# A hybrid encoder trunk on one core: first loads, kept activation sums, an earlier turn and a reshared scaling

## The chip, the core and the metric

The kernel runs on one core of a Trainium2 chip. The metric is the time of one execution in device microseconds (us), taken as the median of several runs. TensorE does the matrix products, VectorE (DVE in the profile), ScalarE (ACT) and GpSimd (POOL) the rest, and SyncE (SP), ACT and POOL issue the DMAs.

## The reference

All tensors are float32. There are 256 positions, the model width is 2048, and there is one layer. Cut to what matters:

```python
def mixer_block(x, ...):
    h = rms_norm(x, g_norm)
    proj = h @ w_in                       # 2048 x 9216: u, v | q, k, v | gates A, B
    uv, qkv, gates = jnp.split(proj, ...)
    y_a = gmlp_branch(uv, ...)            # gelu, LayerNorm of v, spatial mixing of 128 positions, times u
    y_b = neighbourhood_attn(q, k, v, rpb)
    g_a, g_b = jnp.split(jax.nn.sigmoid(gates), 2, axis=-1)
    merged = g_a * (y_a @ w_branch[:GM_WIDTH]) + g_b * (y_b @ w_branch[GM_WIDTH:])
    return x + merged @ w_out

def conv_ffn(x, ...):
    up = rms_norm(x, g_norm) @ w_up       # 2048 x 11008
    up = (pad[:, :t] * conv_k[0] + pad[:, 1:t + 1] * conv_k[1] + pad[:, 2:t + 2] * conv_k[2] + conv_b)
    gate, val = jnp.split(up, 2, axis=-1)
    return x + (jax.nn.silu(gate) * val) @ w_down   # 5504 x 2048

out = rms_norm(conv_ffn(mixer_block(x, ...), ...), norm_final)
```

## The kernel before, in words

**Split products.** Every factor is split in two parts of the type fp32r: a high part (ACT copies it, L151 for weights, tile `whi`) and the rest (DVE subtracts, L152, tile `wlo`). A product is then three matmuls, high by high, low by high and high by low (`triple`, L287 to L291). The activations are split likewise: `x_split` (L493) multiplies the transposed input `xr` by the first norm's gain `gmix`, ACT the high part (L495) and DVE the low one (L496).

**Pieces.** The weights come in pieces of 512 KB, loaded by SP in the order in which they are used, five ahead (`load_to`, L112), and split up to three ahead (`split_to`, L140; four tiles each of `whi` and `wlo`). `begin(i)` (L178) stands ahead of the products of piece `i`: it loads, splits, and runs the tasks that `at(i, f)` has filed under that number. In the first nine pieces the tasks run ahead of the splits and `SPLIT_TO` says how far is split; later the splits come first. A task's instructions stand at that place in each engine's queue, and each engine runs as far ahead as its waits let it.

**Wide groups and seven-product pairs.** A wide group (`run_wide`, L340) makes 1024 output columns for both halves of the positions: four PSUM banks `C[t][c]`, 16 pieces of one 128-row chunk of the weights each. A plain piece is four triples, 12 matmuls. A pair of pieces named in the group's `QUADS` is done by seven products in place of eight, 21 matmuls: DVE adds up blocks of the weights (`weight_sums`, L321, three pieces ahead), ACT and DVE split these (L334, L335, two pieces ahead), and like sums of the activations are needed too (`act_sums`, L300, and `act_sums_split`, L311). Such pairs need four more banks `P`, from the group's first pair to its last, which DVE then reads (`post_sums`); `add_sums` joins both at the group's end. There are eight banks, and a group that takes one waits for the last reader of what was in it.

**Order.** The wide groups are: `g_v` (the gMLP's v, pieces 0 to 15, its order of chunks in `V_ORDER`), `g_va` (attention's v, 16 to 31), then `g_u`, the q and k groups with the first halves of the gates, the branch products (`g_branch`), the second halves of the gates `g_gw[0]` and `g_gw[1]` (pieces 128 to 159), four branch groups `g_m2`, the out projection `g_o` (two wide groups), the up projection and the down projection `g_dn` (two). The first groups' activation sums are made from `xr` (L305), those of the gates again from the split parts (L307). After the second branch's product of a quarter `j`, `ev_branch` (L859) multiplies by the gates (L863) and adds (L866), and `turn_m(j)` (L878) transposes the result: eight TensorE transposes (L885), then ACT and DVE split it (L470, L475).

**Start and end.** Before the first matmuls TensorE runs `WAKE` transposes (L440). The norm's factor is made by `rstd` (L444): the sum (L1187), DVE (L449), a square root on ACT (L450), and five DVE operations. At the end `finish` (L1054) handles one bank of the last group at a time: it adds the residual (L1021), ACT squares it and sums (L1024), DVE multiplies by the last gain (L1061); after the second bank of a half the factor `r` times `e` is made (L1066 to L1072) and `write` (L1074) scales 2048 columns in five parts on DVE (L1083) and ACT (L1081) and stores them in five DMAs (L1087).

Of the kernel before, what the change touches and what calls it, by code (L numbers as in the profile page):

```python
# [8 lines left out]
F32 = mybir.dt.float32  # L9
# [48 lines left out]
Y_GAP = 224  # L58
DOWN_PAIRS = (3, 5, 7, 9, 10, 12, 14, 16, 17, 19)
# [4 lines left out]
def trunk_kernel(ctx, tc, x, x_t, vecs, w_in, ln_g, ln_b, w_st, b_s, rpb, w_branch, w_out, w_up, w_down,  # L64
# [200 lines left out]
    def wide(src, row0, order, c0, acts, quads, room, done, sums=None, odd=None, stored=None, split_room=None):  # L265
        n0 = plan_wide(src, row0, order, c0)
        boxes = {}
        for n, q in enumerate(quads):
            i = n0 + 2 * q
            own = odd if odd and n % 2 else split_room or room  # L270
# [40 lines left out]
    def act_sums_split(box, room, name):  # L311
        w = box.pop("w")
        o = room(name, F32R)
        nc.scalar.activation(o[:, 0], w[:, 1], AF.Copy)
        nc.vector.tensor_sub(o[:, 1], w[:, 1], o[:, 0].bitcast(F32))
        box["s"] = sums_of(o)
# [23 lines left out]
    def run_wide(g, tail=0):  # L340
        kind, n0, order, acts, quads, boxes, done = g
        n1 = n0 + len(order)
        P = C = None

        def x_of(k, t):
            a = acts(k)
            return a[:, 0, t * 128:(t + 1) * 128], a[:, 1, t * 128:(t + 1) * 128]

        def plain(i, t, c):
            h, l = split_t[i]  # L350
            triple(C[t][c], x_of(order[i - n0], t), h[:, c], l[:, c], i == n0, i == n1 - 1)

        for i in range(n0, n1 - tail):
            begin(i)
            q, r = divmod(i - n0, 2)
            if C is None:
                c = [bank() for _ in range(4)]
                C = [c[:2], c[2:]]
            if q not in quads:
                for t, c in ((0, 0), (0, 1), (1, 0), (1, 1)) if i > 1 else ((0, 0), (1, 0), (0, 1), (1, 1)):  # L360
                    plain(i, t, c)
                split_t.pop(i)
                continue
            st, sp = q == quads[0], q == quads[-1]
            k, k1 = order[2 * q:2 * q + 2]
            if r == 0:
                if st:
                    P = [bank() for _ in range(4)]
                (h0, l0), (h1, l1) = split_t[i], split_t[i + 1]
                triple(P[0], x_of(k, 0), h0[:, 0], l0[:, 0], st, sp)  # L370
                triple(C[0][0], x_of(k1, 0), h1[:, 0], l1[:, 0], False, False)
                triple(C[0][1], boxes[q]["acts"]["s"][3], h1[:, 1], l1[:, 1], False, False)
# [7 lines left out]
            triple(C[1][0], x_of(k1, 1), *W[4], False, False)  # L380
# [26 lines left out]
    xr = xin.tile([128, KD, T], F32, name="xr")  # L407
# [5 lines left out]
    def load_xt(k, n, queue=None):  # L413
        (queue or nc.sync).dma_start(xr[:, k:k + n], x_t[:, k:k + n])

    gmix = const.tile([128, KD], F32)
    gffn = const.tile([128, KD], F32)
    ck = const.tile([128, 4, 2 * NF], F32)
    nc.scalar.dma_start(gmix, vecs[:, 0:KD])
    load_xt(1, 1, nc.scalar)  # L420

    def load_late():
        nc.sync.dma_start(gffn, vecs[:, KD:2 * KD])
        nc.sync.dma_start(ck.rearrange("p a b -> p (a b)"), vecs[:, 2 * KD:])
# [19 lines left out]
    def rstd(name, ssum, n, eps):  # L444
        w = ssum.shape[-1]
        a = const.tile([128, w], F32, name=name + "_a")
        r = const.tile([128, w], F32, name=name + "_r")
        s = const.tile([128, w], F32, name=name + "_s")
        nc.vector.tensor_scalar(a, ssum, 1.0 / n, float(eps), op0=OP.mult, op1=OP.add)  # L449
        nc.scalar.activation(s, a, AF.Sqrt)  # L450
        nc.vector.reciprocal(r, s)
# [166 lines left out]

    def mix(g):
        p = bank()  # L620
# [7 lines left out]
        split_plain(y, yT[g])  # L628
# [230 lines left out]
    def ev_branch(br, j):  # L859
        def done(ps, i):  # L860
# [3 lines left out]
            if br == 1:  # L864
                for t in range(NT):
                    nc.vector.tensor_add(g[:, t, :], g[:, t, :], mg[0, j][:, t, :])  # L866
                at(i + 2, lambda: turn_m(j))
# [186 lines left out]
    def finish(ps, t, c):  # L1054
# [7 lines left out]
        if c == 0:  # L1062
            if t:
                fin["out"]()
            return
        a, r, q, e, pt, both = (const.tile([128, 1], F32, name=f"{n}3{t}") for n in "arqepb")  # L1066
        nc.vector.tensor_scalar(pt, fin["ss"][:, t, 2:3], 1.0 / D, fin["part"][:, t:t + 1], op0=OP.mult, op1=OP.add)
        nc.vector.tensor_scalar(a, fin["ss"][:, t, 3:4], 1.0 / D, pt, op0=OP.mult, op1=OP.add)
        nc.scalar.activation(q, a, AF.Sqrt)
        nc.vector.reciprocal(r, q)  # L1070
        nc.vector.scalar_tensor_tensor(e, r, r, a, op0=OP.mult, op1=OP.mult)
        nc.vector.tensor_scalar(e, e, -0.5, 1.5, op0=OP.mult, op1=OP.add)  # L1072

        def write():  # L1074
            on_act = (3,) if t else (1, 3)
            cuts = (0, 256, 768, 1024, 1536, 2048)
            for n in (0, 1, 2, 3, 4):
                v = x2[:, t, cuts[n]:cuts[n + 1]]
                u = y[:, n - 3] if n > 2 else v
                if n in on_act:  # L1080
                    nc.scalar.activation(v, u, AF.Copy, scale=both)  # L1081
                else:
                    nc.vector.tensor_scalar(v, u, r, e, op0=OP.mult, op1=OP.mult)  # L1083
                if n == 0:
                    nc.vector.tensor_mul(both, r, e)
            for n in (0, 1, 2, 3, 4):
                (nc.scalar if n == 3 else nc.sync).dma_start(out[0, t * 128:(t + 1) * 128, cuts[n]:cuts[n + 1]],  # L1087
                                                             x2[:, t, cuts[n]:cuts[n + 1]])
# [15 lines left out]
    def odd_room(name, dt):  # L1104
        return s_room["odd"].tile([128, 2, 512], dt, name=name)

    first_sums = {2 * q: {} for q, _, _ in X_SUMS}
    g_v = wide(w_in2, 0, V_ORDER, V0, xt, V_QUADS, first_room, (ev_v_sums, ev_v), first_sums,
               odd_room)
    g_va = wide(w_in2, 0, VA_ORDER, VA0, xt, VA_QUADS, first_room, (ev_va_sums, ev_va), first_sums)  # L1110
    for n, (q, i, j) in enumerate(X_SUMS):
        sum_acts_at(i, j, first_sums[2 * q], lambda q=q: q,
                    lambda name, dt, i=i: first_room("s2" if name == "f" and i < 9 else name, dt), f"s{n}", True)
# [13 lines left out]
    x_sums, m_sums = ({2 * q: {} for q in qs} for qs in (GATE_PAIRS, OUT_PAIRS))  # L1127
# [5 lines left out]
    for n, q in enumerate(GATE_PAIRS):  # L1133
        i = g_gw[0][1] - 3 + 3 * n
        sum_acts_at(i, i + 1, x_sums[2 * q], lambda q=q: x_pairs[q], sums_room, f"s{n}")
    for n, q in enumerate(OUT_PAIRS):
        i = g_m2[0][1] + 2 + 3 * n
# [29 lines left out]
    dram = keep("dram", space=bass.MemoryType.DRAM)  # L1167
# [9 lines left out]
    for c, i in X_TURN[1:]:  # L1177
        at(i, lambda c=c: x_chunk(c))

    xsq = const.tile([128, NT, 4], F32)  # L1180
# [3 lines left out]

    def x_norm():
        s = const.tile([128, NT], F32, name="ss1")
        nc.vector.tensor_reduce(s, xsq, axis=AX.X, op=OP.add)  # L1187
        r = rstd("n1", s, D, RMS_EPS)
        st1["r"] = r
# [31 lines left out]
    s_room["odd"], odd_st = pool("odd")  # L1221
    at(g_v[1] + 15, odd_st.close)
# [119 lines left out]
```

## Time and profile before

| what | value |
|---|---|
| median of three runs | 1307.59 us (1307.04 to 1307.76) |
| profiled execution, its own time | 1307.19 us |
| its span in the profile | 1305.4 us |
| granted TensorE clock, mean | 0.998 |
| TensorE busy with matmuls | 1292.6 us of the span |
| DVE, ACT, POOL busy | 1082.7, 780.6, 104.7 us |
| moved by DMA | 277.19 MB |

The span runs from the first to the last instruction of the program; 1.8 us of the execution's own time lie around it. Times in the views count from the start of the span. A matmul's end is modelled and the next one starts before it, so what a matmul costs is read from start to start; a line such as "x3" holds several instructions in a row.

### The profile page before, as it was taken

The page shows a single profiled execution, that of the slowest core. Times are in us where ns is not written, and L with a number is a line of the kernel's source. Part 1 is how long each engine was busy: PE and PEld are TensorE (multiplying, and loading weights), DVE is VectorE, ACT ScalarE, POOL GpSimd, SP SyncE. Part 2 cuts the span into 40 slices and gives each one's busy share as a digit, 9 for nine tenths or more (in the row PEclk, how much of TensorE's full clock was granted, in tenths as well). Part 3 has the DMA queues.
Part 4 walks back from the last instruction along what each step waited for, and adds up shares of the span by engine and source line. Part 5 has one row for each costly group of instructions (what it writes and reads, how often), then busy time and mean ns, then how long its engine had stood idle before and what let it go on. Part 6 is the DMA issues. An engine that isn't in the chain of part 4 may idle for free.

```text
span 1305.4 us, 19280 instructions
## 1 busy us (share of the span) xinstructions
PE 1292.6 (99%) x6706; PEld 1102.7 (84%) x6706; DVE 1082.7 (83%) x1634; ACT 780.6 (60%) x1158; POOL 104.7 (8%) x206
## 2 busy tenths in 40 slices
PE   9999999999999999999999999999999999999997
PEld 7888888888888888888888888888888888888885
DVE  7997777677689978897777878787888889999997
ACT  7766476666655644566556556565555656565563
POOL 0006405413000000000000000000000000000000
PEclk9999999999999999999999999999999999999999
DMA  9779656556556656665566666666666758876772
GB/s 357 245 245 267 183 166 214 174 171 194 178 171 203 219 182 242 208 210 164 176 198 206 184 211 195 216 195 214 190 210 199 217 157 290 291 266 226 273 285 104
DMA packets 174225, 277.19 MB, mean 212 GB/s; under 512 B 13488, under 2 KB 121904, under 8 KB 174128
## 3 DMA queue, kind: packets, MB, share of 16 engines
q1 hardware_dynamic: 165520, 252.28, 59.9%
q0 software_dynamic: 8032, 23.03, 5.3%
q8 instruction: 52, 0.85, 0.3%
q10 hardware_dynamic: 576, 0.66, 0.1%
q14 instruction: 45, 0.37, 0.1%
HBM read 266.48 MB, written 7.34 MB: 210 GB/s over the span
## 4 chain that ended last, share of the span: by engine, by line
PE 96%; DVE 2%; ACT 1%; DMA 1%; issue 0%; SPq 0%; ACTq 0%; DVEq 0%
PE bank L203 31%; PE bank L207 16%; PE bank L291 11%; PE bank L289 11%; PE bank L290 11%; PE bank L231 5%; PE bank L233 4%; PE bank L232 4%; DMA wraw<-in_w_in_dram 1%; PE bank L756 1%; DVE wlo L152 0%; PE bank L806 0%; PE bank L622 0%; PE bank L796 0%; PE bank L957 0%
## 5 line engine op out<-in xcount | busy, mean ns | idle before, releaser
L152 DVE TENSOR_TENSOR wlo<-wraw,whi 128x1024 fp32r<-128x1024 f32 (+1 forms) x472 | 545.3, 1169 | 171.7 <-ACT whi L151 93.8
L151 ACT ACTIVATE whi<-wraw 128x1024 fp32r<-128x1024 f32 (+1 forms) x472 | 469.7, 1009 | 207.0 <-PE bank L290 81.3
L203 PE MATMUL bank<-h,whi 128*128 128x512 f32 x1760 | 425.5, 392 | 0.0
L203 PEld LDWEIGHTS bank<-h,whi 128*128 128x128 f32 x1760 | 322.1, 188 | 61.7
L207 PEld LDWEIGHTS bank<-h,wlo 128*128 128x128 f32 x1760 | 225.9, 191 | 8.8
L207 PE MATMUL bank<-h,wlo 128*128 128x256 f32 x1760 | 228.6, 283 | 0.0
L983 ACT ACTIVATE tc<-ta,ck 128x256 f32<-128x256 f32 x86 | 47.1, 595 | 117.7 <-DVE ta L981 117.7
L291 PE MATMUL bank<-wlo,a 128*128 128x512 f32 x224 | 87.3, 390 | 0.0
L289 PE MATMUL bank<-whi,a 128*128 128x512 f32 x224 | 87.2, 389 | 0.0
L290 PE MATMUL bank<-whi,a 128*128 128x512 f32 x224 | 87.2, 389 | 0.0
L290 PE MATMUL bank<-whi,h 128*128 128x512 f32 x210 | 81.9, 390 | 0.8 <-DVE h L496 0.8
L289 PE MATMUL bank<-whi,h 128*128 128x512 f32 x210 | 82.4, 392 | 0.2
L291 PE MATMUL bank<-wlo,h 128*128 128x512 f32 x210 | 82.0, 390 | 0.6 <-DVE wlo L152 0.5
L334 ACT ACTIVATE h<-h 128x1024 fp32r<-128x1024 f32 x40 | 40.2, 1053 | 35.0 <-DVE h L326 35.0
L986 DVE SCALAR_TENSOR_TENSOR tc<-ta,ck,tc 128x255 f32<-128x255 f32 x86 | 41.5, 482 | 14.4 <-ACT tc L983 14.4
L231 PE MATMUL bank<-whi,y 128*128 128x512 f32 x128 | 50.5, 394 | 0.0
L231 PE MATMUL bank<-whi,h 128*128 128x512 f32 x128 | 50.4, 394 | 0.0
L233 PE MATMUL bank<-wlo,h 128*128 128x512 f32 x128 | 49.9, 390 | 0.0
L233 PE MATMUL bank<-wlo,y 128*128 128x512 f32 x128 | 49.9, 390 | 0.0
L232 PE MATMUL bank<-whi,h 128*128 128x512 f32 x128 | 49.9, 389 | 0.0
L232 PE MATMUL bank<-whi,y 128*128 128x512 f32 x128 | 49.8, 389 | 0.0
L291 PEld LDWEIGHTS bank<-wlo,a 128*128 128x128 f32 x224 | 42.0, 188 | 9.1 <-DVE wlo L152 0.3
(290 smaller groups left out, 1800.4 us busy)
## 6 DMA issues: line engine op xcount, KB each, us to landing
wraw<-in_w_up_dram SPq DMA_DIRECT2D x336, 256.0 KB, 3.3
wraw<-in_w_in_dram SPq DMA_DIRECT2D x111, 512.0 KB, 4.3
wraw<-in_w_down_dram SPq DMA_DIRECT2D x86, 512.0 KB, 5.4
wraw<-in_w_in_dram SPq DMA_DIRECT2D x66, 256.0 KB, 3.1
wraw<-in_w_branch_dram SPq DMA_DIRECT2D x32, 512.0 KB, 4.5
wraw<-in_w_out_dram SPq DMA_DIRECT2D x32, 512.0 KB, 4.2
h<-sums POOLq DMA_DIRECT2D x20, 512.0 KB, 6.7
sums<-so POOLq DMA_DIRECT2D x10, 512.0 KB, 5.5
```

The source lines that it names most:

```text
L151: nc.scalar.activation(h[:, k, :m], w[:, k, :m], AF.Copy)
L152: nc.vector.tensor_sub(l[:, k, :m], w[:, k, :m], h[:, k, :m].bitcast(F32))
L203: nc.tensor.matmul(p, h[:, k - k0, b * 128:(b + 1) * 128], acts(k), start=k == 0, stop=k == nk - 1)
L207: nc.tensor.matmul(p[:, :T], l[:, k - k0, b * 128:(b + 1) * 128], acts(k)[:, 0, :], start=False, stop=False)
L231: nc.tensor.matmul(p, xh, h[:, kk, :m], start=st, stop=False)
L232: nc.tensor.matmul(p, xl, h[:, kk, :m], start=False, stop=False)
L233: nc.tensor.matmul(p, xh, l[:, kk, :m], start=False, stop=sp)
L289: nc.tensor.matmul(p, xh, h, start=st, stop=False)
L290: nc.tensor.matmul(p, xl, h, start=False, stop=False)
L291: nc.tensor.matmul(p, xh, l, start=False, stop=sp)
L983: nc.scalar.activation(v, u, AF.Identity, scale=ck[:, 1, ch:ch + 1], bias=ck[:, 3, ch:ch + 1])
L986: nc.vector.scalar_tensor_tensor(v[:, 1:], u[:, :T - 1], ck[:, 0, ch:ch + 1], v[:, 1:], op0=OP.mult, op1=OP.add)
```

## The change

- **First loads.** `gmix` is laid in front of the transposed input in memory and comes with its chunk 0 in one DMA on ACT's queue, with chunk 1 behind it; SP's queue begins with the weights. Chunks 6 and 7 come in a DMA each, ahead of pieces 2 and 3; chunks 2 and 3 come three pieces later than before (and are split two pieces later), chunks 4, 5 and 12 to 15 one. DVE takes the high part of chunk 0. Chunk 6 is split ahead of the weights of piece 2, chunk 7 ahead of those of piece 3. There are 14 `WAKE` transposes in place of 17.
- **First group.** `g_v` has one seven-product pair (pieces 10 and 11) in place of two; the room `odd` goes away. The sums of chunks 2 and 3 are made at pieces 5 and 6 in place of 3 and 4, those of 4 and 5 at 12 and 13 in place of 6 and 9. The norm's sum and root (`x_root`) go ahead of the other tasks of piece 17, the rest (`inverse`) stays behind them.
- **Gates.** `g_gw[0]` has four seven-product pairs, the first at its first piece, `g_gw[1]` three as before, at other places. The activation sums of three pairs are kept: POOL stores the tiles of the first groups to memory (`keep_sums`) and loads them again from four pieces ahead of `g_gw[0]` (`kept_sums`); the fourth is made from the split parts. `first()` marks the first product of a bank, since a pair can now open a group.
- **Turns.** `turn_m(1)` moves from piece 2 of `g_gw[0]` to piece 2 of `g_gw[1]`, `turn_m(3)` from piece 2 of the out projection to its piece 1. The sums for the out projection are made one piece later. In `mix` the split of a result goes to the next piece.
- **End.** The part of the sum that is known after a half's first bank (`p`) is made there, ACT takes the root with the scale and `p` in one instruction, and each half is scaled in four parts (DVE 768 and 512 columns, ACT 512 and 256) and stored in three DMAs.

```diff
-WAKE = 17
-V_QUADS, V_ORDER = ((5, 6), (0, 1, 6, 7, 8, 9, 10, 11, 12, 13, 2, 3, 4, 5, 14, 15))
+WAKE = 14
+V_QUADS, V_ORDER = ((5,), (0, 1, 6, 7, 8, 9, 10, 11, 12, 13, 2, 3, 4, 5, 14, 15))
-X_TURN = ((0, 0), (3, 1), (1, 2), (4, 2), (5, 3), (2, 4), (6, 6), (7, 9))
-SPLIT_TO = (3, 4, 4, 7, 8, 8, 11, 12, 12)
+X_TURN = ((0, 0), (3, 1), (4, 2), (5, 3), (1, 4), (2, 5), (6, 6), (7, 9))
+SPLIT_TO = (2, 4, 4, 7, 8, 8, 11, 12, 12)
-X_SUMS = ((1, 3, 4), (2, 6, 9), (6, 18, 19))
-GATE_PAIRS = (2, 4, 6)
-GATE_QUADS = ((2, 4, 6), (1, 3, 5))
-GATE_ORDER = (tuple(range(16)), (0, 1, 4, 5, 2, 3, 8, 9, 6, 7, 12, 13, 10, 11, 14, 15))
+X_SUMS = ((1, 5, 6), (2, 12, 13), (6, 18, 19))
+GATE_KEPT, GATE_MADE = (1, 2, 6), 4
+GATE_QUADS = ((0, 2, 4, 6), (2, 4, 6))
+GATE_ORDER = ((2, 3, 0, 1, 4, 5, 6, 7, 12, 13, 10, 11, 8, 9, 14, 15), (0, 1, 6, 7, 2, 3, 10, 11, 4, 5, 14, 15, 12, 13, 8, 9))
+KEEP_AT = (22, 25, 29)
...
-    nc.scalar.dma_start(gmix, vecs[:, 0:KD])
+    load_xt(0, 1, nc.scalar)
     load_xt(1, 1, nc.scalar)
...
     def x_split(k):
         a, g = xT[k], gmix[:, k:k + 1]
-        nc.scalar.activation(a[:, 0, :], xr[:, k], AF.Copy, scale=g)
+        if k:
+            nc.scalar.activation(a[:, 0, :], xr[:, k], AF.Copy, scale=g)
+        else:
+            nc.vector.tensor_scalar(a[:, 0, :], xr[:, k], g, None, op0=OP.mult)
...
-        split_plain(y, yT[g])
+        gm_pool["last"] = lambda: split_plain(y, yT[g])
+        at(cur[0] + 1, end_mix)
...
-                at(i + 2, lambda: turn_m(j))
+                at(i + 1 if j == 3 else g_gw[1][1] + 2 if j == 1 else i + 2, lambda: turn_m(j))
...
-        nc.vector.tensor_scalar(pt, fin["ss"][:, t, 2:3], 1.0 / D, fin["part"][:, t:t + 1], op0=OP.mult, op1=OP.add)
-        nc.vector.tensor_scalar(a, fin["ss"][:, t, 3:4], 1.0 / D, pt, op0=OP.mult, op1=OP.add)
-        nc.scalar.activation(q, a, AF.Sqrt)
+        nc.scalar.activation(q, ss, AF.Sqrt, scale=1.0 / D, bias=pt)
+        nc.vector.tensor_scalar(a, ss, 1.0 / D, pt, op0=OP.mult, op1=OP.add)
...
+        nc.vector.tensor_mul(both, r, e)
...
+            for u, w in ((v[:, :768], v[:, :768]), (y[:, 1], v[:, 1536:])):
+                nc.vector.tensor_scalar(w, u, r, e, op0=OP.mult, op1=OP.mult)
+            for u, w in ((y[:, 0], v[:, 1024:1536]), (v[:, 768:1024], v[:, 768:1024])):
+                nc.scalar.activation(w, u, AF.Copy, scale=both)
+            nc.sync.dma_start(o[:, :768], v[:, :768])
+            nc.sync.dma_start(o[:, 1536:], v[:, 1536:])
+            nc.scalar.dma_start(o[:, 768:1536], v[:, 768:1536])
...
+    def x_root():
+        s = const.tile([128, NT], F32, name="ss1")
+        nc.vector.tensor_reduce(s, xsq, axis=AX.X, op=OP.add)
+        st1["root"] = root("n1", s, D, RMS_EPS)
+    def x_norm():
+        st1["r"] = inverse(*st1["root"])
+    at(NORM_AT, x_root)
...
+    def keep_sums(q):
+        nc.gpsimd.dma_start(x_kept[q], first_sums[2 * q]["tile"].bitcast(F32))
+    def kept_sums(n, q):
+        o = sums_room(f"s{n}", F32R)
+        nc.gpsimd.dma_start(o.bitcast(F32), x_kept[q])
+        x_sums[2 * q]["s"] = sums_of(o)
+    for n, q in enumerate(GATE_KEPT):
+        at(KEEP_AT[n], lambda q=q: keep_sums(q))
+        at(g_gw[0][1] - 4 + n, lambda n=n, q=q: kept_sums(n, q))
+    sum_acts_at(g_gw[0][1] - 1, g_gw[0][1] + 1, x_sums[2 * GATE_MADE], lambda: x_pairs[GATE_MADE], sums_room, "s3")
...
-        i = g_m2[0][1] + 2 + 3 * n
+        i = g_m2[0][1] + 3 + 3 * n
...
-    preload[0] = [lambda: load_xt(0, 1)]
-    for n, (c, _) in enumerate(X_TURN[1:]):
-        preload[n + 2] = [lambda c=c: load_xt(2 * c, 2)]
+    first_chunk = X_TURN[1][0]
+    preload[2] = [lambda: load_xt(2 * first_chunk, 1)]
+    preload[3] = [lambda: load_xt(2 * first_chunk + 1, 1)]
+    for n, (c, _) in enumerate(X_TURN[2:]):
+        preload.setdefault(n + 4, []).append(lambda c=c: load_xt(2 * c, 2))
...
+    at(1, lambda: x_split(2 * first_chunk))
+    at(1, lambda: split_to(3))
+    at(1, lambda: x_split(2 * first_chunk + 1))
```

More of the change, by code (lines that the diff above doesn't have):

```diff
@@ L260, in run_group, with wide @@
             done(ps, b)
-    def wide(src, row0, order, c0, acts, quads, room, done, sums=None, odd=None, stored=None, split_room=None):
+    def wide(src, row0, order, c0, acts, quads, room, done, sums=None, stored=None, split_room=None):
         n0 = plan_wide(src, row0, order, c0)
         boxes = {}
-        for n, q in enumerate(quads):
+        for q in quads:
             i = n0 + 2 * q
-            own = odd if odd and n % 2 else split_room or room
+            own = split_room or room
             whole[i] = whole[i + 1] = None
@@ L343, in run_wide, with first @@
         P = C = None
+        begun = set()
+        def first(t, c):
+            new = (t, c) not in begun
+            begun.add((t, c))
+            return new
         def x_of(k, t):
@@ L350, in plain @@
             h, l = split_t[i]
-            triple(C[t][c], x_of(order[i - n0], t), h[:, c], l[:, c], i == n0, i == n1 - 1)
+            triple(C[t][c], x_of(order[i - n0], t), h[:, c], l[:, c], first(t, c), i == n1 - 1)
         for i in range(n0, n1 - tail):
@@ L370, in run_wide @@
                 triple(P[0], x_of(k, 0), h0[:, 0], l0[:, 0], st, sp)
[L371 to L372 removed]
+                triple(C[0][0], x_of(k1, 0), h1[:, 0], l1[:, 0], first(0, 0), False)
+                triple(C[0][1], boxes[q]["acts"]["s"][3], h1[:, 1], l1[:, 1], first(0, 1), False)
                 split_t.pop(i)
@@ L379, in run_wide @@
             triple(P[2], S[2], *W[2], st, sp)
-            triple(C[1][0], x_of(k1, 1), *W[4], False, False)
+            triple(C[1][0], x_of(k1, 1), *W[4], first(1, 0), False)
             if sp:
@@ L617, in combine, with end_mix @@
         return outs
+    def end_mix():
+        gm_pool.pop("last", lambda: None)()
     def mix(g):
+        end_mix()
         p = bank()
@@ L1072, in finish @@
         nc.vector.tensor_scalar(e, e, -0.5, 1.5, op0=OP.mult, op1=OP.add)
+        nc.vector.tensor_mul(both, r, e)
         def write():
[L1075 to L1088, printed above, removed]
+            v = x2[:, t]
+            o = out[0, t * 128:(t + 1) * 128]
+            for u, w in ((v[:, :768], v[:, :768]), (y[:, 1], v[:, 1536:])):
[5 more added lines that the diff above has]
+            nc.scalar.dma_start(o[:, 768:1536], v[:, 768:1536])
         if t:
```

62 lines of the change are left out of this document (29 added, 33 removed).

## The prediction

> **What bounds the kernel now.** I read the page first, then TensorE's waits, then the timelines around each of them.
>
> ```profile
> span 1305.4 us, 19280 instructions
> PE 1292.6 (99%) x6706; PEld 1102.7 (84%) x6706; DVE 1082.7 (83%) x1634; ACT 780.6 (60%) x1158; POOL 104.7 (8%) x206
> PE 96%; DVE 2%; ACT 1%; DMA 1%; issue 0%; SPq 0%; ACTq 0%; DVEq 0%
> PE bank L289 <- DVE m L475: 0.8, 1, 0.8
> PE bank L290 <- DVE h L496: 0.8, 1, 0.8
> PE bank L291 <- DVE wlo L152: 0.5, 1, 0.5
> 507.92 0.39 PE L289 MATMUL bank<-whi,m 128*128 128x512 f32 x1
> 510.63 0.39 PE L289 MATMUL bank<-whi,m 128*128 128x512 f32 x1
> ```
>
> TensorE sets the time: 96% of the chain, and few waits. The last two rows are the starts of two neighbouring plain pieces: 2.71 us for 12 matmuls, 0.226 us from start to start. So a change pays where it takes matmuls away, where it takes one of the few stalls away, or at the two ends. A view counts only the idle time after a matmul's modelled end; I take a stall as start to start less 0.23.
>
> Matmuls: `g_v` loses a seven-product pair (three matmuls more, 3 x 0.226 = 0.68 us), `g_gw[0]` gains one (0.68 less). Together nothing. What is left are stalls.
>
> **First loads.**
>
> ```profile
> 1.37 3.89 PE L440 MATMUL bank<-ident 128*128 128x128 f32 x17 [1.37 <-POOL ident masks.py:199]
> 4.64 0.63 ACT L151 ACTIVATE whi<-wraw 128x512 fp32r<-128x512 f32 x1 [0.93 <-DMA wraw<-in_w_in_dram]
> 5.33 0.76 PE L289 MATMUL bank<-whi,h 128*128 128x512 f32 x1
> 6.16 0.40 PE L291 MATMUL bank<-wlo,h 128*128 128x512 f32 x1
> 9.99 1.06 ACT L151 ACTIVATE whi<-wraw 128x1024 fp32r<-128x1024 f32 x1 [2.15 <-DMA wraw<-in_w_in_dram]
> 11.08 1.23 DVE L152 TENSOR_TENSOR wlo<-wraw,whi 128x1024 fp32r<-128x1024 f32 x1 [2.44 <-ACT whi L151]
> 12.22 0.88 DVE L496 SCALAR_TENSOR_TENSOR h<-xr,gmix,h 128x256 fp32r<-128x256 f32 x2
> 13.10 0.40 PE L291 MATMUL bank<-wlo,h 128*128 128x512 f32 x1
> 18.37 0.39 PE L290 MATMUL bank<-whi,h 128*128 128x512 f32 x1
> 18.85 0.50 PE L291 MATMUL bank<-wlo,h 128*128 128x512 f32 x1
> 6.00:21.00 15.00, 14.00 (x59) 10.66 (x58) 12.14 (x23) 12.32 (x22) 0.00 (x0) 1.00 1.03 401
> ```
>
> Two things make the stalls: piece 2's weights land at 9.99 (the ACT row is released by the DMA), and chunk 6 is split behind them (12.22), so that the second product starts late and the third, at 13.10, later still. At 18.37 a third product waits 0.25 for `wlo`, held up on DVE by the early activation sums.
>
> After: the weights are first on SP's queue, and less goes ahead of them. The first matmul followed 0.69 behind the ACT row at 4.64; the chunk that was ahead of them now takes turns with them from ACT's queue, where another followed it before; some 110 KB less by then, at 300 to 400 GB/s, is 0.35, so it comes at about 4.98. Up to piece 2's weights there are 128 KB less (one chunk in place of two), at the 401 GB/s of the last row 0.33; with the gain's many tiny rows gone I take 0.44: they land at 9.55. Then `whi` to 10.6, `wlo` (1.23) to 11.9, third product at 11.95. Without any wait it would come 26 products and some 0.5 for the slow first ones behind 4.98, at 11.4, so a stall of 0.55 stays, where the weights now come last and not the chunk. Against 13.10 that is 1.15. The stall at 18.37, 0.25 and 0.11 in the next start, goes too: `wlo` of piece 4 is, by the same durations, ready at 16.95 and wanted at 17.4. Sum 1.5. Bounds: weights no earlier than before, 1.0; no stall left at all, 2.1. DVE's high part of chunk 0 costs nothing, since DVE waits there anyway until 5.3; if that cover were gone, 0.4.
>
> [...]
>
> **The first group's end.**
>
> ```profile
> 54.57 0.69 DVE L324 TENSOR_TENSOR y<-wraw 128x512 f32<-128x512 f32 x1
> 57.49 0.20 ACT L450 ACTIVATE n_s<-n_a 128x2 f32<-128x2 f32 x1 [4.36 <-DVE n_a L449]
> 61.08 0.91 ACT L305 ACTIVATE y<-xr,gmix 128x256 f32<-128x256 f32 x2 [0.53 <-DVE y L335]
> 64.45 1.04 ACT L151 ACTIVATE whi<-wraw 128x1024 fp32r<-128x1024 f32 x1
> 65.54 0.50 PE L289 MATMUL bank<-whi,h 128*128 128x512 f32 x1
> 65.52 1.22 DVE L152 TENSOR_TENSOR wlo<-wraw,whi 128x1024 fp32r<-128x1024 f32 x1 [2.29 <-ACT whi L151]
> 66.80 0.50 PE L291 MATMUL bank<-wlo,h 128*128 128x512 f32 x1 [0.53 <-DVE wlo L152]
> ```
>
> Piece 22 starts at 65.54 and its third product only at 66.80 in place of 65.99: with the slower starts around it 0.9 us. Read back: `wlo` waits for `whi`, ACT is late since it waited 4.36 us for `n_a`, and DVE made that behind four weight sums (from 54.57, 2.5 us). After, `x_root` goes ahead of those sums, and the pair that is gone leaves DVE nothing to catch up. TensorE is by now 1.5 - 0.68 = 0.82 earlier, and so is the half `whi` of piece 20, which waits for it: 51.8 to 52.4. From there on DVE: `wlo` to 53.05, root 0.4, weight sums to 55.95, inverse 0.95, `wlo` 1.15, first L335 1.15, so L305 on ACT can start at 59.2 (before: 61.08); from it to the end of the gelu 3.4 as before (61.08 to 64.45), then `whi` 1.05 and `wlo` 1.2: done at 64.9, wanted at 65.2. Gain 0.8, with only 0.3 to spare; bounds 0.3 and 0.9. The kept sums' stores are POOL's and wait only for their tiles, so they run at about 24, 40 and 65 us, not at 22, 25 and 29 pieces; nothing is queued behind them on POOL that is due before 100 us. As DMA they delay later weights by 1.3 us each, which lie 1.5 us or more ahead of their use.
>
> **Gates.**
>
> ```profile
> 361.69 0.69 PE L806 MATMUL bank<-pT,vw 128*64 128x64 f32 x16
> 371.66 1.23 DVE L152 TENSOR_TENSOR wlo<-wraw,whi 128x1024 fp32r<-128x1024 f32 x1 [0.56 <-ACT whi L151]
> 379.19 1.35 DVE L863 TENSOR_TENSOR g<-bank,g 128x512 f32<-128x512 f32 x2
> 379.65 0.39 PE L289 MATMUL bank<-whi,h 128*128 128x512 f32 x1
> h<-sums POOLq DMA_DIRECT2D x20, 512.0 KB, 6.7
> ```
>
> `g_gw[0]` starts at 379.65, without a stall. Now a pair opens it. Weight sums (four adds, 54.57 to 57.1 above, 2.5) and their split (two of 1.2) come ahead of the branch's L863 at 379.19, less half a `wlo` and one 0.6 split: L863 moves some 3 us to 382.2, the first bank free at 382.9. The group now takes all eight banks in its first two pieces. In what order, the wait at 517.95 (below) shows: there the fourth matrix `P[3]`, third to be written, started when two of the four L475 (517.05 to 518.46) were done, so it had the turn's first bank: banks go by first use. Then the ones that L863 frees are the last two, wanted 18 products in, at 383.7. Cost 0, with 0.8 to spare; if the order were that of the code, the fourth would be wanted at 382.4 and come at 383.55: 1.2. The kept sums are loaded from four pieces ahead (368); at 6.7 us they land by 375, wanted at 381. The moved `turn_m(1)` is wanted 32 pieces later: 0. In `mix`, TensorE doesn't wait: 0.
>
> **The turn for the out projection.**
>
> ```profile
> 508.97 1.28 DVE L863 TENSOR_TENSOR g<-bank,g 128x512 f32<-128x512 f32 x2
> 510.17 1.28 DVE L866 TENSOR_TENSOR g<-g,g 128x512 f32<-128x512 f32 x2
> 513.36 1.03 PE L885 MATMUL bank<-ident,g 128*128 128x128 f32 x8
> 517.05 1.41 DVE L475 TENSOR_TENSOR m<-bank,m 128x256 fp32r<-128x256 f32 x4
> 517.95 0.47 PE L289 MATMUL bank<-h,s 128*128 128x512 f32 x1 [0.82 <-DVE m L475]
> ```
>
> The stall at 517.95 is 1.0 us, a bank that the turn's split frees late. A piece earlier it is free in time. But the transposes then stand in TensorE's queue at 510.63, and the second of them needs both additions of L866, done at 511.45; DVE is late with them since weight sums go ahead. All matmuls of piece 1 queue behind: 0.7. Gain 0.3; bounds 0 (the additions later still) and 1.0 (if they are in time).
>
> **The end.**
>
> ```profile
> 1298.10 0.21 DVE L1068 TENSOR_SCALAR a<-ss,p 128x1 f32<-128x1 f32 x1
> 1298.35 0.20 ACT L1069 ACTIVATE q<-a 128x1 f32<-128x1 f32 x1 [0.28 <-DVE a L1068]
> 1299.23 0.41 DVE L1083 TENSOR_SCALAR x<-x,r,e 128x256 f32<-128x256 f32 x1
> 1301.11 0.41 SPq L1087 DMA_DIRECT2D out_dram<-x  x1
> ```
>
> The root starts at 1298.10 in place of 1298.35. The first part is 768 columns wide and `both` goes ahead of it, so the first store leaves about 0.1 later, the last at 1300.3 in place of 1301.11. Most of the 1 MB's transfer lies behind the first store, so I take 0.3 of the 0.8; bounds -0.3 and 0.7.
>
> **Sum.** 1.5 + 0.8 + 0 + 0.3 + 0.3 = 2.9, so 1307.19 - 2.9 = 1304.3 for the profiled execution; that one lies 0.4 below the median, and against the median it is 1304.7. The least of the terms together: 1.0 + 0.3 - 1.2 + 0 - 0.3 = -0.2, the most: 2.1 + 0.9 + 1.0 + 0.7 = 4.7, or 1307.8 and 1302.9.
>
> **Rivals.** (1) Less gain: the gate group's banks come as in the code, or the chain to piece 22 keeps its stall: 1.2 or 0.5 less, 1305.2 to 1305.9. For it: DVE is full there (wlo at 371.66 waited only 0.56). Against: the wait at 517.95 tells the order. [...] (3) More gain: additions of L866 in time, weights early: 4.4 and up, 1303.2. (4) Slower: the kept sums come late at 381. Place: the third matmul triple of `g_gw[0]`. If the memory under their tiles, used by the attention before, comes free only at 380 or the load meets the weights at full queues, each us past 381 is a us; past 383.9 the gain is gone, and a whole 6.7 us load after the group's start gives 386.4, 5.4 lost, 1310.1. Against: the attention's last products are 18 us earlier.
>
> **How the numbers follow.** 0.2% is 2.6 us, about what a measurement of this kernel can tell from no change; the line is at 1304.97. Forecast (1304.0 to 1305.3) 0.50, of it 0.38 beyond the line; more gain 0.28; less gain 0.08 and the wake 0.04, both within 0.2%; slower 0.10, of it 0.09 beyond. Faster 0.38 + 0.28 = 0.66, same 0.12 + 0.08 + 0.04 + 0.01 = 0.25, slower 0.09. The range takes in the wake and the bounds: 1302.7 to 1307.4.
>
> **What would show it.** Right: first matmul near 5.0, piece 2's third product near 12, no wait at 66.8 less 1.7, a new wait of TensorE on L866 of some 0.7 at the turn, none on `s`, last store near 1300.3 less the gains. Wrong: a wait of L289 on L863 or on the kept sums' DMA at the first gate group, products at half pace past 6.2, or a first matmul no earlier than 5.3.

## The result

| | median | from - to | beside it: the kernel before |
|---|---|---|---|
| changed kernel, 7 executions | 1303.26 us | 1302.95 - 1303.95 | 1307.88 us (1307.04 - 1308.34), 7 executions |
| the same once more, 6 executions | 1303.19 us | 1303.10 - 1303.51 | 1307.46 us (1306.86 - 1308.64), 15 executions |

The ratio is 0.9966 (95% interval 0.9955 to 0.9978), the second time 0.9968 (0.9957 to 0.9980): faster by 0.3%, 4.6 and 4.3 us between the medians. The prediction had 2.9.

The profiled execution of the changed kernel is the slowest of its seven (1303.95). The second series has a profile of its own (1303.21); below, "after" is the first and "control" the second. From the page and from TensorE's waits of after:

```profile
span 1302.2 us, 19268 instructions
PE 1291.6 (99%) x6703; PEld 1102.0 (85%) x6703; DVE 1078.2 (83%) x1620; ACT 780.2 (60%) x1156; POOL 108.9 (8%) x212
PE 99%; DVE 1%; ACT 0%; issue 0%; POOL 0%; POOLq 0%; ACTq 0%
PE bank L205 <- DVE ya L646: 0.6, 1, 0.6
PE bank L906 <- DVE g L887: 0.3, 1, 0.3
```

The three waits of the kernel before (0.8 for the turn, 0.8 for chunk 6, 0.5 for `wlo`) are gone; there is the small one on L887 that was foreseen, and one on L646 that was not. From the timeline of after, the start:

```profile
1.37 3.25 PE L450 MATMUL bank<-ident 128*128 128x128 f32 x14 [1.37 <-POOL ident masks.py:199]
3.95 0.63 ACT L153 ACTIVATE whi<-wraw 128x512 fp32r<-128x512 f32 x1 [0.78 <-DMA wraw<-in_w_in_dram]
4.63 0.79 PE L291 MATMUL bank<-whi,h 128*128 128x512 f32 x1
8.31 0.49 ACT L509 ACTIVATE h<-xr 128x256 fp32r<-128x256 f32 x1
9.13 1.06 ACT L153 ACTIVATE whi<-wraw 128x1024 fp32r<-128x1024 f32 x1 [0.32 <-DMA wraw<-in_w_in_dram]
10.22 1.23 DVE L154 TENSOR_TENSOR wlo<-wraw,whi 128x1024 fp32r<-128x1024 f32 x1 [0.61 <-ACT whi L153]
11.52 0.48 PE L293 MATMUL bank<-wlo,h 128*128 128x512 f32 x1
```

Chunk 6 is now split ahead of piece 2's weights (8.31), these come at 9.13 in place of 9.99, and the third product follows at 11.52 in place of 13.10, with no stall. The end of the first group, in the same timeline:

```profile
52.93 0.20 ACT L457 ACTIVATE n_s<-n_a 128x2 f32<-128x2 f32 x1 [1.03 <-DVE n_a L456]
58.61 0.91 ACT L307 ACTIVATE y<-xr 128x256 f32<-128x256 f32 x2 [1.66 <-DVE y L337]
63.06 1.23 DVE L154 TENSOR_TENSOR wlo<-wraw,whi 128x1024 fp32r<-128x1024 f32 x1 [2.29 <-PE bank L293]
64.67 0.39 PE L293 MATMUL bank<-wlo,h 128*128 128x512 f32 x1
```

`n_s` waits 1.03 in place of 4.36, and the third product of piece 22 runs at its pace. The turn:

```profile
506.77 1.28 DVE L884 TENSOR_TENSOR g<-bank,g 128x512 f32<-128x512 f32 x2
507.97 1.28 DVE L887 TENSOR_TENSOR g<-g,g 128x512 f32<-128x512 f32 x2
508.71 0.33 PE L906 MATMUL bank<-ident,g 128*128 128x128 f32 x1
509.31 0.98 PE L906 MATMUL bank<-ident,g 128*128 128x128 f32 x7 [0.27 <-DVE g L887]
513.71 1.42 DVE L488 TENSOR_TENSOR m<-bank,m 128x256 fp32r<-128x256 f32 x4
```

The transposes stand in TensorE's queue from 508.4 and wait for both additions: 0.77 from start to start, in place of 1.0 before. The end:

```profile
1295.42 0.30 ACT L1091 ACTIVATE q<-ss,p 128x1 f32<-128x1 f32 x1
1295.42 0.21 DVE L1092 TENSOR_SCALAR a<-ss,p 128x1 f32<-128x1 f32 x1
1297.17 0.33 SPq L1105 DMA_DIRECT2D out_dram<-x  x1
1297.63 0.35 SPq L1106 DMA_DIRECT2D out_dram<-x  x1
1297.74 0.35 ACTq L1107 DMA_DIRECT2D out_dram<-x  x1
```

The root starts beside `a`, and the last store is issued 3.84 behind the last matmul's end (1293.90), where it was 4.69 (1301.11 less 1296.42).

Both kernels have 6689 matmuls behind the waking transposes, so the k-th of one (counted from 0) can be set against the k-th of the other: for good, the difference of their starts changes only where one of them stalls.

| lead over the kernel before, us | after | control | predicted for the stretch |
|---|---|---|---|
| at the 60th (21.25 before): the start | 1.91 | 1.77 | 1.5 |
| at the 300th (76.68): piece 22 | 2.94 (+1.03) | 2.80 (+1.03) | +0.8 |
| at the 2250th (439.70): attention, gates | 2.20 (-0.74) | 2.93 (+0.13) | 0 |
| at the 2700th (540.96): the turn | 2.47 (+0.27) | 3.20 (+0.27) | +0.3 |
| last matmul's end (1296.42) | 2.51 | 3.24 | |
| from there to the span's end, 8.99 before | 8.26 (+0.73) | 8.26 (+0.73) | +0.3 |

For the control 3.24 and 0.73 are 4.0, the difference between the profiled execution before and its own (1307.19 less 1303.21).

### The profile page after: what moved, and what is told of

Read it like the earlier page. It is cut to its first block, busy times and chain, and to the rows that moved or that the text cites. A ratio compares the mean times of both kernels' runs of the same rounds, so it can differ in the third digit from the quotient of the medians.

```text
span 1302.2 us, 19268 instructions
## 1 busy us (share of the span) xinstructions
PE 1291.6 (99%) x6703; PEld 1102.0 (85%) x6703; DVE 1078.2 (83%) x1620; ACT 780.2 (60%) x1156; POOL 108.9 (8%) x212
## 4 chain that ended last, share of the span: by engine, by line
PE 99%; DVE 1%; ACT 0%; issue 0%; POOL 0%; POOLq 0%; ACTq 0%
PE bank L205 31%; PE bank L209 16%; PE bank L291 12%; PE bank L293 12%; PE bank L292 12%; PE bank L233 4%; PE bank L234 4%; PE bank L235 4%; PE bank L777 1%; PE bank L827 0%; PE bank L906 0%; PE bank L642 0%; PE bank L978 0%; PE bank L817 0%; PE bank L450 0%
## 5 line engine op out<-in xcount | busy, mean ns | idle before, releaser
L1029 POOL DMA_DIRECT2D sums<-so x10 | 5.4, 538 | 548.1 <-DVE so L494 459.8
```

## Experiments

The theory (A): the gain is TensorE's stalls that go, each worth its length, and nothing else. Its rivals are named with each run. The kernel of each run is the changed one with the edit shown, but for the one that says otherwise. The reference for medians is the second series, 1303.19. The kernel before was measured beside every run, and its median moves from series to series: 1307.46 beside the control, the late root, the made sums and 17 transposes; 1307.90 beside `mix`, the old loads, the old scaling and the additions first; 1307.67 beside the root alone, 8 transposes and the later pair; 1307.31 beside both edits together. So a median from another series is compared by its gain over the kernel before beside it; the control's gain is 4.3.

**The wait at 137 us: `mix` splits at once again.**

```diff
-        gm_pool["last"] = lambda: split_plain(y, yT[g])
-        at(cur[0] + 1, end_mix)
+        split_plain(y, yT[g])
```

> `mix` splits its result at once again, as in the kernel before; all else as after. Theory A (what the change gains is stalls of TensorE that go, less the one that it makes): the wait of 0.6 us for L646 at 137 us, start to start 0.85, is gone, and from there on every matmul comes 0.85 earlier: 1302.4 as a median against 1303.26. Rival R1 (the stall at 137 us is made by the earlier weights, not by the split's place): the wait stays and the time is 1303.3.

Measured 1303.80 (1303.40 to 1304.23), a gain of 4.1: not faster. The wait is gone from its profile, but the expected 0.85 did not come. Its last matmul ends at 1293.33, the control's, which splits late, at 1293.18. So the wait isn't the split's.

**The changed kernel again.**

> The changed kernel itself once more, unchanged, beside the others of this call. Theory A (the start is not the same in every execution: with the same instructions the first half of the first weights landed at 3.93 us in the profile of after and at 4.19 to 4.45 in three kernels that share its first loads, and the wait of 0.6 at 137 us was met in one of them only, the earliest): the median is between 1303.0 and 1304.0, and the profile has the wait at 137 us only if its first product comes before 4.8. Rival R5 (the wait at 137 us belongs to the split put off in `mix`): it is there in this profile too, whatever the start.

1303.19, and no wait at 137; the first product came at 4.87. The same instructions with and without the wait, so R5 falls. From the timelines of after and then of control:

```profile
120.28 1.06 ACT L153 ACTIVATE whi<-wraw 128x1024 fp32r<-128x1024 f32 x1 [2.08 <-DMA wraw<-in_w_in_dram]
136.57 1.32 DVE L154 TENSOR_TENSOR wlo<-wraw,whi 128x1024 fp32r<-128x1024 f32 x1 [0.47 <-ACT whi L153]
137.81 0.48 DVE L646 TENSOR_TENSOR ya<-bank,bsb 128x128 f32<-128x128 f32 x2
138.34 2.35 PE L205 MATMUL bank<-h,whi 128*128 128x512 f32 x9 [0.58 <-DVE ya L646]
```

```profile
118.00 1.06 ACT L153 ACTIVATE whi<-wraw 128x1024 fp32r<-128x1024 f32 x1 [3.29 <-DMA wraw<-in_w_in_dram]
134.30 1.32 DVE L154 TENSOR_TENSOR wlo<-wraw,whi 128x1024 fp32r<-128x1024 f32 x1 [0.47 <-DMA wraw<-in_w_in_dram]
135.54 0.48 DVE L646 TENSOR_TENSOR ya<-bank,bsb 128x128 f32<-128x128 f32 x2
136.13 4.72 PE L205 MATMUL bank<-h,whi 128*128 128x512 f32 x20
```

DVE is 2.27 later in after, TensorE 0.14 earlier. Followed back, the 2.27 is there since 120 us, where ACT waits for a load of weights in both: issued at 107.03 it landed at 120.19, in the control issued at 107.17 it landed at 117.92, among the 128 KB transfers of `vw` (the DMA engines are 99% busy from 100 to 118 us). The wait is met again in the kernel before with an early root (below), whose load of that place landed at 121.22, where it landed at 119.85 in the kernel before, and whose `mix` is the old one. Why the same load lands later in one execution than in another isn't shown.

**The first loads as before.** 17 transposes, the old order, queues and places of splitting; the new places of the early activation sums stay.

```diff
-WAKE = 14
+WAKE = 17
-X_TURN = ((0, 0), (3, 1), (4, 2), (5, 3), (1, 4), (2, 5), (6, 6), (7, 9))
-SPLIT_TO = (2, 4, 4, 7, 8, 8, 11, 12, 12)
+X_TURN = ((0, 0), (3, 1), (1, 2), (4, 2), (5, 3), (2, 4), (6, 6), (7, 9))
+SPLIT_TO = (3, 4, 4, 7, 8, 8, 11, 12, 12)
...
-    load_xt(0, 1, nc.scalar)
+    nc.scalar.dma_start(gmix, x_t[:, :KD])
...
+    preload[0] = [lambda: load_xt(0, 1)]
```

> The first loads as in the kernel before: 17 transposes, gain and second chunk on ACT's queue, first chunk ahead of the weights on SP's, pairs of chunks in the old order, high part of the first chunk on ACT, weights' third low part split as before; all else as after. Theory A: first matmul at 5.3 in place of 4.6, third product of piece 2 at 13.1 in place of 11.5, and the 1.9 us of the start come back: 1305.1. Rival R2 (the later root of the first group covers it: an earlier start only waits longer at piece 22): the stall near 66 us eats it, and it is at most 0.9 slower, 1303.3 to 1304.2.

1304.86 (1304.37 to 1305.35), a gain of 3.0: 1.2 slower than the control. The stall of piece 2 is back, and the 60th product comes at 20.64 in place of 19.48, 1.16 later:

```profile
11.31 0.51 PE L291 MATMUL bank<-whi,h 128*128 128x512 f32 x1
12.57 0.50 PE L292 MATMUL bank<-whi,h 128*128 128x512 f32 x1 [0.75 <-DVE h L509]
```

It is less than the 1.9 expected, as the stall at 18.4 stays away: that one didn't go with the loads but with what this run keeps, most likely the later places of the early sums (0.38 of the lead comes between the 48th and the 60th product, here as in the control). R2 falls: nothing later gives the start back, as the last matmul's end is 1.19 behind the control's.

**The last scaling as before.** The old function `finish` in place of the new one.

> The last scaling as in the kernel before (five cuts, five stores for each half of the rows, the root behind its sum); all else as after. Theory A: from the last matmul's end to the span's end 9.0 us in place of 8.3, so 0.7 slower: 1304.0, and nothing ahead of the last matmul moves. Rival R3 (the end is the transfer of the last megabyte, however it is cut, and the 0.7 is a difference from run to run): 8.3 stays, 1303.3.

1304.07 (1303.80 to 1304.43), a gain of 3.8: 0.4 slower by the medians. The trace is clearer: the last matmul's end to the span's end is 8.99 again (1293.49 to 1302.48), 0.73 more than with the new scaling. That stretch is 8.24 to 8.29 in all eleven profiles with the new scaling and 8.99 to 9.01 in the three with the old one, so R3 falls. The root, the cuts and the stores were not undone apart, so what each is worth isn't shown.

**The root late again, and early alone.** First in the changed kernel:

```diff
-    at(NORM_AT, x_root)
...
+    at(NORM_AT, x_root)
     at(NORM_AT, x_norm)
```

> The root of the first normalisation behind the weight sums again, at the place of the kernel before; all else as after. Theory A (the order on DVE made the stall at the end of the first group): TensorE waits for `wlo` at piece 22 again, 0.7 to 1.0: 1304.1. Rival R7 (the pair that is gone relieves DVE enough, the order matters little): no such wait, 1303.3.

1303.41 (1303.25 to 1306.03), 0.2 slower: the lead grows at piece 22 by 0.79 still (1.79 to 2.58), where it was 1.03. Rival R7 is nearer: most of the gain is there without the new order. Then the kernel before with that order as its only edit:

> The kernel before with one part of the change alone: the root of the first normalisation is begun ahead of the weight sums, its inverse stays where it was. Theory A2 (as the prediction's step had it, the order on DVE makes the stall at the end of the first group): `n_s` comes some 2.7 us earlier on ACT, the stall of 0.9 to 1.0 near 66 us goes, 1306.8 against 1307.8. Rival R9 (the order is worth only the 0.25 that its absence cost in the changed kernel; the rest is the pair that is gone, whose sums and splits held DVE up): 0.2 to 0.4 of the stall goes, 1307.4.

1307.40 against 1307.67 beside it, ratio 0.9997 (0.9989 to 1.0006): not to be told from no change. The timeline shows the order at work:

```profile
54.74 0.21 ACT L450 ACTIVATE n_s<-n_a 128x2 f32<-128x2 f32 x1 [1.81 <-DVE n_a L449]
60.41 0.91 ACT L305 ACTIVATE y<-xr,gmix 128x256 f32<-128x256 f32 x2 [1.74 <-DVE y L335]
66.14 0.50 PE L291 MATMUL bank<-wlo,h 128*128 128x512 f32 x1 [0.28 <-DVE wlo L152]
```

`n_s` is 2.75 earlier, L305 only 0.67, since it now waits for `y` from DVE; the lead grows by 0.46 at piece 22. So without the new order the rest of the change is worth 0.79 there, the order alone 0.46, both together 1.03. A2 falls as the whole cause. The rest is most likely the pair that is gone, but the moved sums and the earlier start came with it and were not tried apart.

**The gates without kept sums.** The three sums of `GATE_KEPT` are made again, one a piece from four pieces ahead.

```diff
-        at(KEEP_AT[n], lambda q=q: keep_sums(q))
-        at(g_gw[0][1] - 4 + n, lambda n=n, q=q: kept_sums(n, q))
+        i = g_gw[0][1] - 4 + n
+        sum_acts_at(i, i + 1, x_sums[2 * q], lambda q=q: x_pairs[q], sums_room, f"s{n}")
```

> The three kept sums of the gates are worked out again, one a piece from four pieces ahead of the first gate group, in place of stored and loaded; the pair that moved stays moved. Theory A: DVE has hardly a gap from 364.7 on, so three times 2.45 us of sums put L884 and the `wlo` behind them some 5 to 7 us later, of which the lead of the splits hides 2 to 4: TensorE waits 2 to 4 us at the first gate group, 1305.3 to 1307.3; so the kept sums pay for the seventh pair at the gates. Rival R8 (the lead of the splits hides all of it): 1303.3, and the stores and loads bring nothing.

1313.31, ratio 1.0046 (1.0032 to 1.0060): 10 slower, where A had 2 to 4. From its waits, and from its windows (length, then busy time and, in brackets, instructions of TensorE and the other engines; the granted clock is third from the end):

```profile
PE bank L291 <- DVE m L488: 2.7, 1, 2.7
PE bank L291 <- DVE g L884: 2.4, 1, 2.4
```

```profile
390.00:395.00 5.00, 5.00 (x13) 3.83 (x13) 4.96 (x9) 0.56 (x1) 0.00 (x0) 0.50 0.29 74
397.00:402.00 5.00, 5.00 (x24) 4.12 (x23) 5.00 (x6) 3.74 (x5) 0.00 (x0) 1.00 0.62 188
```

L884, at 380.51 after, starts at 388.87 (some 1.1 of it is a later start of the whole execution); both the turn's split and the branch's products free their banks late. From start to start the two waits cost 5.7 of the 9.2 that the lead loses at the gates. The rest goes with the clock: from 385.39 to 395.63 the trace has it granted at half, and the products start 0.43 apart in place of 0.23. So the waits cost more than their length here, which theory A leaves out. And at these places the pair can stand at the gates only with the kept sums.

**The turn: additions first.** The first weight sums of the out projection a piece later.

```diff
-            at(i - 3, lambda i=i, b=b: weight_sums(i, b, room))
-            at(i - 2, lambda b=b, own=own: weight_sums_split(b, own))
+            d = q in late
+            at(i - 3 + d, lambda i=i, b=b: weight_sums(i, b, room))
+            at(i - 2 + d, lambda b=b, own=own: weight_sums_split(b, own))
```

(with `late=(1,)`, the first pair, for the first of the two groups of the out projection)

> The first weight sums of the out projection a piece later, so that the additions of L887 come ahead of them on DVE; all else as after. Theory A (the second transpose waits for additions that stand behind four weight sums): the wait at 509 us goes, 0.5 to 0.75 faster than after: 1302.6, and the turn's whole stall of the kernel before is gone. Rival R4 (the sums are then late themselves): TensorE waits for a sums' part `h` or `l` at the second half of the first pair, some 3 pieces on, by 1 to 2 us: 1303.6 to 1304.6.

1303.80 (1303.23 to 1305.52), a gain of 4.1. Its timeline:

```profile
507.85 1.29 DVE L888 TENSOR_TENSOR g<-g,g 128x512 f32<-128x512 f32 x2
509.77 1.03 PE L907 MATMUL bank<-ident,g 128*128 128x128 f32 x8
513.85 2.35 DVE L338 TENSOR_TENSOR l<-t,h 128x1024 fp32r<-128x1024 f32 x2
516.12 1.41 DVE L489 TENSOR_TENSOR m<-bank,m 128x256 fp32r<-128x256 f32 x4
517.02 0.47 PE L292 MATMUL bank<-h,s 128*128 128x512 f32 x1 [0.76 <-DVE m L489]
```

The transposes no longer wait, but the sums' split now stands ahead of the turn's, and the old stall of the kernel before is back (0.92). R4 had the wait moving to a part of the sums; it moved to the turn's split.

**The turn: the pair later.** So both lists must go apart.

```diff
-OUT_QUADS = ((1, 3, 5), (1, 3, 5))
+OUT_QUADS = ((2, 4, 5), (1, 3, 5))
-OUT_ORDER = ((6, 7, 0, 1, 8, 9, 2, 3, 10, 11, 4, 5, 12, 13, 14, 15),) * 2
+OUT_ORDER = ((6, 7, 8, 9, 0, 1, 10, 11, 2, 3, 4, 5, 12, 13, 14, 15), (6, 7, 0, 1, 8, 9, 2, 3, 10, 11, 4, 5, 12, 13, 14, 15))
```

> In the first out projection group the seven-product pairs stand at places 2, 4, 5 in place of 1, 3, 5, all else as after: the first weight sums come two pieces later, behind the additions that the turn's transposes wait for, and the four banks of a pair are first wanted two pieces later. Theory A (the turn's stall is nothing but the order of that work): the wait for L887 at 508 us goes and the old one for the turn's split doesn't come back: 0.7 to 0.8 less, 1302.4. Rival R11 (DVE has too little room there, the wait only moves): two neighbouring pairs cost 2 x 2.5 us of sums and 2 x 2.35 of splits within two pieces, and TensorE waits there for a sums' part, 0.8 or more: 1303.2 to 1304.5.

1302.57 (1302.30 to 1303.89), ratio 0.9961 (0.9949 to 0.9974), a gain of 5.1. The additions (506.07) and the turn's split (511.77) are both in time:

```profile
506.07 1.28 DVE L887 TENSOR_TENSOR g<-g,g 128x512 f32<-128x512 f32 x2
507.99 1.03 PE L906 MATMUL bank<-ident,g 128*128 128x128 f32 x8
511.77 1.41 DVE L488 TENSOR_TENSOR m<-bank,m 128x256 fp32r<-128x256 f32 x4
```

The lead grows by 1.10 at the turn, where the change alone had 0.27. R11 falls.

**Fewer and more transposes.** `WAKE` alone, 17 and 8.

> 17 transposes in place of 14; all else as after. Theory A (the transposes only have to reach to the first product): they end 0.7 later, at 5.3, so the first products come 0.1 to 0.7 later, which piece 2's weights hide in part: 1303.3 to 1303.7, and no execution is 1.5 or more above the others, as two of the seven of the kernel with the additions first were (1305.5), whose profile has the products at 0.43 in place of 0.23 us until 10.9. Rival R6 (the clock doesn't depend on the transposes, the late products come from the loads): the same spread as with 14.

1303.27 (1303.04 to 1303.65): the three transposes less are worth nothing at the median.

> 8 transposes in place of 14, all else as after: the last of them starts at 2.8, and 1.9 to 2.4 us without work lie ahead of the first product. Theory A3 (the transposes bring the clock up, and a pause ahead of the products lets it miss the stretch in which it rises): the products run at 0.43 until 9 to 11 in every execution, and the 34th product after piece 2 comes 1.5 to 2.1 later, as in the two disturbed starts seen so far (21.3 and 21.6 in place of 19.5): 1304.9 to 1305.3. Rival R10 (the transposes don't count; the slow starts come from elsewhere): as with 14, 1303.2 in most executions and 1305.5 in some.

1304.29 (1304.05 to 1305.81), a gain of 3.4: 0.9 slower than the control. A3 was too sharp: six of nine lie at 1304.05 to 1304.47, three at 1305.10 to 1305.81, and the profiled one is the last of these. TensorE's timeline in the run with the additions first (14 transposes) shows what such a start is:

```profile
5.04 0.79 PE L292 MATMUL bank<-whi,h 128*128 128x512 f32 x1 [0.41 <-ACT whi L153]
7.08 0.63 PE L293 MATMUL bank<-whi,h 128*128 128x512 f32 x1
7.51 0.63 PE L294 MATMUL bank<-wlo,h 128*128 128x512 f32 x1
10.89 0.40 PE L293 MATMUL bank<-whi,h 128*128 128x512 f32 x1
11.12 0.40 PE L294 MATMUL bank<-wlo,h 128*128 128x512 f32 x1
```

0.43 from start to start until 10.5, then 0.23; the 60th product at 21.56 in place of 19.48. Such a start costs 2.1 us there. The granted clock says the same. The trace has it on record at full only from 10.83 in this run, from 9.93 in the run with the made sums and from 11.29 with 8 transposes, and in each that is where 0.43 gives way to 0.23; in the other eight profiles with these loads it is from 4.09 to 6.01. (A windows row that lies ahead of the first record reads 1.00 all the same.)

With 14 transposes and these loads, 6 of 52 executions lie 0.9 to 2.6 above their kernel's median, and the two of these that were profiled both show it.

**Both edits together.** The later pair and 17 transposes.

> The pairs of the out projection at places 2, 4, 5 as in the run before, and 17 transposes in place of 14: the two edits that the runs so far speak for. Theory A (the later pair takes the turn's 0.77 away; the longer wake costs nothing at the median and shuts out the starts at half pace, of which the kernels with 14 transposes and the same loads had some 6 in 47 executions): 1302.5 as a median, all executions within 1.0 of each other. Rival R12 (the half pace comes with late loads whatever the number of transposes): the same median, and one or more executions 1.3 to 2.5 above it.

1302.56 (1302.20 to 1302.91), ratio 0.9963 (0.9949 to 0.9976); no stall of 0.4 or more is left between the first products and the end. With 17 transposes and these loads none of 11 executions (this and the one with 17 alone) lies over 0.4 above its median. That speaks for the longer wake; with 6 in 52 to compare it doesn't prove it. Nor is the pause ahead of the first product alone the cause: with 14 transposes it was 1.0 us in the profile of the later pair (4.42 to 5.46) and no start at half pace followed, while in the run with the additions first, whose start was slow, it was only 0.4 us (4.63 to 5.04). It is the version I would keep: in the traces 0.83 better at the turn, while the intervals of the ratios overlap with that of the change.

## Why the prediction was right, and where not

The direction and most of the waits came as foretold, but the size didn't: the forecast was 1304.0 to 1305.3, and 1303.26 lies below it. The start, the first group's end and the last scaling each brought more than was said.

- **Start, 1.5; measured 1.77 to 1.91.** In the control the loads give 1.39 where the prediction had 1.15, the sums 0.38 where it had 0.36. The mis-sized term is the stall of 0.55 that was to stay at piece 2: its weights came at 9.13, not at 9.55, and the stall didn't exist. A second size was off the other way: the slow first products cost about 1.0 and not 0.5 (11.52 less 4.63 less 26 times 0.226). So the third product, at 11.52 and 11.77, came not far ahead of the foretold 11.95 although no weights held it up. Undone, the loads cost 1.2.
- **First group's end, 0.8; measured 1.03.** Size nearly right, cause half right. The step put it on the root's order and gave the pair a half sentence; without the order 0.79 is left, and the order alone gives 0.46.
- **Pairs and gates, 0; measured 0.1 in the control.** No wait on L884 or on a kept sum. That the kept sums are what makes it 0 was left unsaid: without them it is 10.
- **Turn, 0.3; measured 0.27**, with the wait on L887 at 0.77 where 0.7 was said.
- **The end, 0.3; measured 0.73, and 0.73 again when undone.** The step "most of the 1 MB's transfer lies behind the first store, so I take 0.3 of the 0.8" failed: the first store left 3.27 behind the last matmul's end, much as before (3.25), the last issue came 0.85 earlier, and nearly all of that reached the span's end.
- **`mix`, 0: right**, although the profile of after seemed to refute it.
- The sum: 2.9 foretold; 4.0 between the profiled executions of the kernel before and of the control, which has no wait at 137, and 3.2 to that of after, which has it. The rest of the 4.6 between the medians is that the profiled execution before lay 0.7 below the median of seven.

The 0.04 that the chances give to the wake, and its part of the range, rest on nothing that a run shows. What the runs showed in its place: with 14 transposes and these loads 6 of 52 executions lie 0.9 to 2.6 above their kernel's median, and the start of one of them in the traces is 2.1 late at the 60th product (21.56 in place of 19.48).

Of the rivals, the late kept sums (4) did not come: they landed at 373.5 at the latest and were wanted from 379.5. "More gain" (3) gave the right time, but only half of its reason came: the weights were early, the additions were not in time; the rest is the end.

At the start the slow products differ in number from trace to trace, with 14 transposes in both: three in after (starts 4.63 to 5.65, each 0.34 to 0.59 ahead of the next), 13 in the run with the additions first (5.04 to 10.49, 0.40 to 0.60). In the profile of the later pair the full clock is on record from 4.09, when TensorE had done nothing but transposes (the first product came at 5.46), and with 8 in place of 14 the gain is 0.9 less.

The kernel that splits at once in `mix` has a median 0.6 above the control while its matmuls end within 0.15 of it in the profiles; 0.44 of that is the series, since the kernel before was that much slower beside it. Open: what the six better executions with 8 transposes look like, since the profiled one is of the other kind; and what makes a start at half pace with 14.

## What to carry to other kernels

When TensorE is busy 99% of the span, list its stalls by start to start and price each edit by the stall that it ends, then by the next thing in line: at the turn one edit only changed which wait came last, another moved it, and only giving both chains room ended it. Before a new wait in a profile is explained, look at the same kernel a second time: one that hangs on when a transfer lands may be there in one execution and not in the next (here 0.58 us where the load landed at 120.19, none where it landed at 117.92). At the end of this kernel it was the issue of the last store that counted (0.85 earlier, for 0.73 at the span's end), not of the first. And a median belongs to its series: set it against a kernel measured beside it, and take terms under 1 us from start to start in the traces.

## What the runs showed of the hardware

- The first load of weights, the same instruction issued at 0.75, landed between 3.93 and 4.76 us in the kernels with the new loads (first product 4.63 to 5.46); the third product of piece 2 came at 11.5 to 12.1 where the products ran at their pace, and piece 2's weights landed at 8.6 to 9.3 there.
- The half pace of the products goes with the granted clock: with the made sums it was 0.50 from 390 to 395 us, with 13 matmuls in that stretch, and 1.00 from 397 to 402, with 24.
- There it came behind a single wait: TensorE was idle for 2.73 us ahead of 384.79, the clock was granted at half from 385.39, and it stayed so for 10.2 us, over a second wait of 2.42.
- With 14 or 17 transposes ahead the full clock is on record from 4.09 to 7.49 us in eleven of thirteen profiles, in one of them ahead of the first product; in the other two, both with 14, it came at 9.93 and 10.83.
- In the stretch from 103 to 117 us of after, where the share of the DMA engines is 1.02 at 222 GB/s, with seven transfers of 128 KB and five of 31.2 KB beside five loads of 512 KB, the load of 512 KB issued at 103.5 us took 13.6 us in after and 9.6 in the control, the same kernel, against a median of 4.6 over the 111 loads of that kind.
